# Projecting pairs of weight chunks by seven block products instead of eight in a three-branch decoder layer

## The chip, the cores and the metric

The kernel runs on one core of one Trainium2 chip. The metric is the time of one execution on the device in microseconds (us); lower is better. Engines are named as the profile names them: PE is TensorE's matmuls (PEld its weight loads), DVE is VectorE, ACT is ScalarE, POOL is GpSimd, SP is the engine from whose queue nearly all DMAs are issued.

## The reference

One decoder layer on 2048 tokens of width 1024, with 16 meta tokens in front: three causal mixers with four heads of 128 side by side, each gated and projected back.

```python
xn = rms_norm(h, norm_w)
proj = jnp.einsum('btd,dn->btn', xn, w_in)          # 1024 -> 9224 columns
(sb_q, sb_k, sb_v, sb_z, gd_qkv, gd_z, gd_b, gd_a,
 hg_q, hg_f, hg_i, hg_z, mix) = jnp.split(proj, split_points, axis=-1)
...
o_sb = stick_breaking_attention(q, k, v, valid) * silu(sb_z)
o_gd = rms_norm(gated_delta_rule_chunked(l2_norm(gq), l2_norm(gk), gv, beta, g)) * silu(gd_z)
o_hg = rms_norm(hgrn2_chunked(silu(hg_q), hk, hg_i, log(forget))) * silu(hg_z)
y = sum over b of sigmoid(mix[b]) * (o_b @ w_branch[b])
return h + y @ w_out
```

All inputs are float32.

## The kernel before, in words

The 2048 tokens are worked through in four quarters of 512 columns (`TQ`); the first also carries the 16 meta tokens (`META`), so its tiles are 528 wide (`WQ`). Activations lie with features on the partitions: eight tiles of 128 features for the normed input.

*Dense work* is a Python generator (`dense_work`). For each quarter it projects 73 chunks of 128 output columns of `w_in` (`proj`): per head four for the attention (k, q, v, gate), one small chunk for beta and decay (`CH_BA`), twelve convolved ones and four gates for the delta rule, sixteen for HGRN2, and 24 mix gates, the latter mixed with the branch products (`branch`: four heads x 1024 outputs for each of three branches). At the end stands the output projection (`outp`, eight chunks).

Each float32 operand is held as a high and a low part of type float32r, and a product of two is three matmuls (`mm3`: high x high, high x low, low x high, lines 147 to 149). A chunk is 8 x 3 matmuls of 512 columns into one PSUM bank; in the first quarter, chunks that also need the meta tokens run in two halves of 264. Weights come from HBM in blocks of 128 x 512 (`load_w`): in the first quarter the raw block is loaded, ACT casts the high part (line 136), DVE or POOL subtracts to get the low part (line 110), and both parts are stored to a DRAM scratch (`wk`, 512 KB); later quarters read that (line 132). The tiles for it are `w2` (five buffers) and `wraw` (two).

*Scans* are generators too: the attention scan per head (`sb_scan`), preparation and scan of the delta rule (`gdn_mats`, `gdn_scan`), and the HGRN2 scan, two heads at a time (`hg_scan`). `weave` runs a scan beside a number of dense steps; both yield estimates of time, by which it interleaves them. `later` puts small follow-up steps of a projection (transposes, sums over features) behind the next chunk. The order so written is the priority order of the tile scheduler, which sets each engine's final sequence and the buffers; each engine then runs its sequence in order, waiting on semaphores.

PSUM has eight banks: three for `acc` (dense work), four for `z` and `tr` (scans), one for `av` (the attention's accumulator). SBUF's wide tiles come in tags: `D` (18 buffers, dense results), `S` (21, scans), `g`, `y`, `ob`. The gated sum `y` over the branches stays in SBUF between branches.

## Time and profile before

| | |
|---|---|
| median of 3 runs | 2871.85 us (2870.64 to 2877.4) |
| the profiled execution's own time | 2878.11 us |
| its span, first to last instruction | 2876.0 us |
| instructions | 42134 |
| granted TensorE clock, mean | 0.993 |
| DMA, packets and data | 198288 packets, 522.74 MB |
| HBM | 399.13 MB read, 120.84 MB written |

Busy time of an engine is the sum of its instructions' durations; matmuls are pipelined, so that of PE overlaps itself, and the rate of matmuls is read from the spacing of their starts. A window's row gives its length, the busy time of each engine with the instructions in it, the granted clock, the DMA engines' mean busy share and what they moved in GB/s. A row of waits reads: who, at which line, waited for whom; us in total, how many times, the longest. A row of a group reads: line, engine, operation, out<-in, shapes, count, then busy us and mean ns of one, then the engine's idle time before them and what ended it.

### The profile page before, as it was taken

The page shows a single profiled execution, that of the slowest core. Times are in us where ns is not written, and L with a number is a line of the kernel's source. Part 1 is how long each engine was busy: PE and PEld are TensorE (multiplying, and loading weights), DVE is VectorE, ACT ScalarE, POOL GpSimd, SP SyncE. Part 2 cuts the span into 40 slices and gives each one's busy share as a digit, 9 for nine tenths or more (in the row PEclk, how much of TensorE's full clock was granted, in tenths as well). Part 3 has the DMA queues.
Part 4 walks back from the last instruction along what each step waited for, and adds up shares of the span by engine and source line. Part 5 has one row for each costly group of instructions (what it writes and reads, how often), then busy time and mean ns, then how long its engine had stood idle before and what let it go on. Part 6 is the DMA issues. An engine that isn't in the chain of part 4 may idle for free.

```text
span 2876.0 us, 42134 instructions
## 1 busy us (share of the span) xinstructions
PE 2786.5 (97%) x15691; PEld 2325.4 (81%) x15691; DVE 1524.5 (53%) x3069; ACT 932.1 (32%) x2123; POOL 760.0 (26%) x1012
## 2 busy tenths in 40 slices
PE   5999999998999999999999999999999999999999
PEld 4898788886788888888888888888888777787887
DVE  4467637635257543654156855555415677627521
ACT  4555233333245312113045531211314555121110
POOL 4556213333123401212022421111302233302111
PEclk9999999999999999999999999999999999999999
DMA  6667655667754664446754456344674443653546
GB/s 203 237 214 230 230 193 189 227 233 260 252 170 148 193 181 133 139 153 226 227 190 163 155 161 186 106 142 147 227 227 147 141 139 125 197 155 103 155 153 212
DMA packets 198288, 522.74 MB, mean 182 GB/s; under 512 B 40448, under 2 KB 41536, under 8 KB 198084
## 3 DMA queue, kind: packets, MB, share of 16 engines
q1 hardware_dynamic: 197796, 519.98, 55.6%
q8 instruction: 124, 2.03, 0.3%
q14 instruction: 80, 0.66, 0.1%
q10 hardware_dynamic: 288, 0.07, 0.0%
HBM read 399.13 MB, written 120.84 MB: 181 GB/s over the span
## 4 chain that ended last, share of the span: by engine, by line
PE 81%; DVE 7%; DMA 6%; ACT 2%; POOL 2%; issue 1%; SPq 1%; ACTq 0%; DVEq 0%; POOLq 0%
PE acc L147 21%; PE acc L149 21%; PE acc L148 20%; DMA wraw<-in_w_in_dram 2%; PE z L1011 2%; PE tr L445 2%; PE acc L276 1%; PE av L147 1%; PE av L148 1%; PE av L149 1%; PE z L147 1%; PE z L149 1%; PE z L148 1%; DVE D L178 1%; DMA wraw<-in_w_out_dram 1%
## 5 line engine op out<-in xcount | busy, mean ns | idle before, releaser
L147 PE MATMUL acc<-xh,w 128*128 128x512 f32 (+1 forms) x2568 | 989.8, 386 | 15.4 <-ACT w L136 4.1
L149 PE MATMUL acc<-xh,w 128*128 128x512 f32 (+1 forms) x2568 | 974.6, 380 | 0.4 <-POOL w L110 0.4
L148 PE MATMUL acc<-xl,w 128*128 128x512 f32 (+1 forms) x2568 | 966.6, 376 | 7.9 <-DVE xl L110 7.9
L147 PEld LDWEIGHTS acc<-xh,w 128*128 128x128 f32 x2568 | 486.9, 190 | 97.0 <-ACT w L136 4.2
L148 PEld LDWEIGHTS acc<-xl,w 128*128 128x128 f32 x2568 | 487.5, 190 | 88.1 <-DVE xl L110 8.4
L149 PEld LDWEIGHTS acc<-xh,w 128*128 128x128 f32 x2568 | 485.6, 189 | 85.6 <-POOL w L110 0.8
L110 POOL TENSOR_TENSOR w<-wraw,w 128x512 fp32r<-128x512 f32 x110 | 145.4, 1323 | 346.7 <-ACT w L136 327.9
L136 ACT CAST w<-wraw 128x512 fp32r<-128x512 f32 x186 | 115.0, 618 | 251.9 <-DMA wraw<-in_w_in_dram 104.8
L421 POOL TENSOR_TENSOR S<-S,S 128x256 f32<-128x256 f32 (+2 forms) x108 | 95.2, 882 | 382.9 <-DVE S L413 217.5
L413 DVE TENSOR_TENSOR_SCAN S<-S,cc,zero 128x272 f32<-128x272 f32 (+2 forms) x152 | 144.1, 948 | 82.2 <-ACT S L407 81.7
L147 PE MATMUL acc<-ob,w 128*128 128x512 f32 x384 | 156.4, 409 | 11.9 <-DVE D L1083 5.5
L407 ACT ACTIVATE S<-z,rq 128x128 f32<-128x128 f32 (+4 forms) x216 | 116.8, 541 | 129.1 <-PE z L149 95.2
L148 PE MATMUL acc<-ob,w 128*128 128x512 f32 x384 | 153.4, 400 | 0.0
L149 PE MATMUL acc<-ob,w 128*128 128x512 f32 x384 | 152.3, 397 | 0.0
L592 DVE SCALAR_TENSOR_TENSOR D<-D,cw,D 128x512 f32<-128x512 f32 (+1 forms) x144 | 125.2, 869 | 23.1 <-ACT D L590 20.7
L110 DVE TENSOR_TENSOR S<-tr,S 128x512 fp32r<-128x512 f32 (+4 forms) x176 | 105.1, 606 | 39.8 <-ACT S L449 39.1
L1085 POOL TENSOR_TENSOR y<-y,g 128x512 f32<-128x512 f32 x32 | 49.7, 1558 | 285.8 <-DVE g L1083 285.8
L1067 ACT ACTIVATE g<-acc 128x512 f32<-128x512 f32 x64 | 38.3, 598 | 261.9 <-PE acc L149 247.2
L116 POOL TENSOR_SCALAR nu<-nv 128x8 f32<-128x8 f32 (+4 forms) x40 | 15.3, 383 | 397.2 <-DVE nv L888 231.1
L408 ACT ACTIVATE S<-z,rq 128x128 f32<-128x128 f32 (+4 forms) x216 | 116.3, 538 | 0.0
L449 ACT CAST S<-tr 128x512 fp32r<-128x512 f32 (+4 forms) x176 | 91.0, 529 | 59.4 <-PE tr L445 58.1
L445 PE MATMUL tr<-ident,S 128*128 128x128 f32 (+1 forms) x608 | 100.9, 273 | 3.9 <-POOL S L421 3.2
(325 smaller groups left out, 4700.7 us busy)
## 6 DMA issues: line engine op xcount, KB each, us to landing
w<-wk SPq DMA_DIRECT2D x558, 512.0 KB, 3.5
wk<-w SPq DMA_DIRECT2D x186, 512.0 KB, 2.9
wraw<-in_w_in_dram SPq DMA_DIRECT2D x146, 256.0 KB, 3.8
D<-in_xq_dram SPq DMA_DIRECT2D x56, 256.0 KB, 4.7
S<-rows SPq DMA_DIRECT2D x48, 256.0 KB, 4.5
S<-dv SPq DMA_DIRECT2D x48, 256.0 KB, 4.5
out_dram<-D SPq DMA_DIRECT2D x32, 256.0 KB, 4.7
S<-dk SPq DMA_DIRECT2D x24, 264.0 KB, 4.0
```

Source lines behind the costliest of these rows:

```text
L110: (eng or nc.gpsimd).tensor_sub(out_, a, hi.bitcast(F32))
L136: nc.scalar.copy(hi, raw)
L147: nc.tensor.matmul(dst, lh, rh, start=first, stop=False)
L148: nc.tensor.matmul(dst, lh, rl, start=False, stop=False)
L149: nc.tensor.matmul(dst, ll, rh, start=False, stop=last)
L407: nc.scalar.activation(pc[:, :n], z[:, :n], AF.Sigmoid, scale=rq[:, NT + i : NT + i + 1])
L408: nc.scalar.activation(at[:, :n], z[:, :n], AF.Sigmoid, scale=rq[:, i : i + 1])
L413: nc.vector.tensor_tensor_scan(pc[:, 0:n][:, ::-1], pc[:, 0:n][:, ::-1], zero1.broadcast_to([P, n]), 1.0 if carry[i] is None else carry[i] ...
L421: eng.tensor_mul(at[:, :n], at[:, :n], pc[:, 1 : n + 1])
L445: nc.tensor.transpose(tr[:kw, i * P : (i + 1) * P], ats[i][:, a - lo : a - lo + kw], ident)
L449: nc.scalar.copy(ath[:kw, cs_], tr[:kw, cs_])
L592: nc.vector.scalar_tensor_tensor(dst[:, c0:], raw[:, c0 + i : c0 + i + n], cw[:, ci, i : i + 1], dst[:, c0:], ALU.mult, ALU.add)
```

## The change

*Pairs of chunks in later quarters.* `proj` is replaced by `proj2`, which takes two chunks a and b. Seen as a product of 2 x 2 blocks (inputs 0 to 511 and 512 to 1023; chunk a and chunk b; tokens in two halves of 256), it needs eight block products. In quarters two to four seven are made, by Winograd's scheme: of blocks of weights 11, 12, 22 and four sums of blocks S1 to S4, with blocks of the input 11, 21, 22 and four sums t1 to t4. Each product is 4 x 3 matmuls of 256 columns into its own PSUM bank, with its own weight tile.

*Sums.* `norm_x` makes the input's sums once per quarter and splits all seven blocks. `sums_w` makes S1 to S4 in the first quarter, after a pair has been projected plainly (`proj2_plain`, eight products in halves of 264 for all chunks), and stores their high and low parts. Blocks 11, 12 and 22 are stored only for the attention and delta-rule chunks (`all_kept`); for the others later quarters load them raw and split them again, on ACT and POOL.

*Evacuation.* The products are combined out of PSUM: one ACT copy, then DVE additions (`total`, `sum_to`) into small tiles `u` (256 columns, five buffers); activations then read those. Some gate multiplications and scalings go to POOL.

*Buffers.* PSUM: four banks for `acc`, and `av` shares the four of `z`. SBUF: one set of 47 wide slots serves `D`, `S`, `g`, `y` and `ob`; `y` goes to DRAM and back between branches; the delta rule's inversion takes a `w2` tile and a `u` tile, its output reuses `gq`; HGRN2's `AT` tiles come from the slots.

*Order.* `later` takes the number of ticks after which a step is due; the attention's keys and values of an earlier quarter are fetched one quarter ahead; the small chunk holds its high and low parts side by side in one weight tile and uses two matmuls per block; the counts and costs for `weave` are new.

```diff
-    ps_acc = ctx.enter_context(tc.tile_pool(name="ps_acc", bufs=3, space=PSUM))
+    ps_acc = ctx.enter_context(tc.tile_pool(name="ps_acc", bufs=4, space=PSUM))
     ps_z = ctx.enter_context(tc.tile_pool(name="ps_z", bufs=4, space=PSUM))
-    ps_av = ctx.enter_context(tc.tile_pool(name="ps_av", bufs=1, space=PSUM))
...
+    WIDE = {"D", "S", "g", "y", "ob"}
+    N_WIDE = 47
...
+    def pair_w(ca, cb, j):
+        a1, a2, b2 = w_in[ca][:, :512], w_in[ca][:, 512:], w_in[cb][:, 512:]
+        for src, key in ((a1, "11"), (a2, "12"), (None, "S2"), (None, "S3"), (None, "S1"), (b2, "22"), (None, "S4")):
+            key = (ca, key)
+            yield parts(kept_w(key) if key in kept else split_w(w_raw(src), j))
...
+    def sums_w(ca, r11, r12, r21, r22):
+        w_eng(0).tensor_add(r22, r21, r22)
+        w_eng(0).tensor_sub(r21, r11, r21)
+        w_eng(0).tensor_sub(r11, r22, r11)
+        w_eng(0).tensor_sub(r12, r12, r11)
+        for i, (name, v) in enumerate((("S3", r21), ("S1", r22), ("S2", r11), ("S4", r12))):
+            w2 = spare(4 + i % 2)
+            nc.scalar.copy(w2[:, 0], v)
+            sub_lo(w2[:, 1], v, w2[:, 0], w_eng(0))
+            d_ = dram.tile([P, 2, 512], F32, name=nm("wk"))
+            nc.sync.dma_start(d_, w2.bitcast(F32))
+            kept[ca, name] = d_
...
+    def proj2(j, xs, ca, cb, meta, eva, evb, mid=True):
...
+        def prod(dst, name):
+            wh, wl = nxt[0]
+            nxt[0] = next(gen, None)
+            xh, xl = xs[name]
+            for k in range(4):
+                mm3(dst, wh[:, k], wl[:, k], xh[:, k], xl[:, k], k == 0, k == 3)
...
+        ps = bank()
+        yield from prod(ps, "11")
+        p1 = side()[:, :n]
+        nc.scalar.copy(p1, ps)
+        p2 = bank()
+        yield from prod(p2, "21")
+        give(eva, p1, p2, ha)
+        p6 = bank()
+        yield from prod(p6, "t2")
+        u2 = total(p1, p6)
+        p7 = bank()
+        yield from prod(p7, "t3")
+        u3 = total(u2, p7)
...
+        yield from prod(p5, "t1")
+        give(evb, u3, p5, hb)
+        nc.vector.tensor_add(u2, u2, p5)
+        p4 = bank()
+        yield from prod(p4, "t4")
+        give(evb, u3, p4, ha)
+        p3 = bank()
+        yield from prod(p3, "22")
+        give(eva, u2, p3, hb)
```

Three places in the third quarter's second branch show what moves; names are tiles with their numbers. First PE, at the first mix gates, before: one chunk, `acc_18329` its bank, `w` a weight tile, `xh` and `xl` the input's parts.

```order
L147 MATMUL acc_18329<-xh_13558,w_3822_18325 128x512
L148 MATMUL acc_18329<-xl_13559,w_3822_18325 128x512
L149 MATMUL acc_18329<-xh_13558,w_3822_18325 128x512
L147 MATMUL acc_18329<-xh_13563,w_3822_18325 128x512
L148 MATMUL acc_18329<-xl_13564,w_3822_18325 128x512
L149 MATMUL acc_18329<-xh_13563,w_3822_18325 128x512
```

The same engine and place now, from the end of the fifth of the seven products on:

```order
L230 MATMUL acc_24368<-xh_17876,w_4916_24352 128x256
L228 MATMUL acc_24390<-xh_17882,w_4920_24371 128x256
L229 MATMUL acc_24390<-xl_17883,w_4920_24371 128x256
L228 MATMUL acc_24408<-xh_17874,w_4923_24391 128x256
L229 MATMUL acc_24408<-xl_17875,w_4923_24391 128x256
L230 MATMUL acc_24408<-xh_17874,w_4923_24391 128x256
L228 MATMUL acc_24408<-xh_17874,w_4923_24391 128x256
```

Matmuls are half as wide, a bank and a weight tile change after twelve of them, and the sixth product, whose weights are split again from a raw block (`w_4920`), is left after two matmuls for the seventh and finished after it.

Then DVE, at the same gates, before (lines 981 to 1020 are the HGRN2 scan; the gate itself is evacuated by ACT, and L1083 multiplies a branch product by it):

```order
L981 TENSOR_TENSOR S_18543<-D_18218,D_18183 128x32x8
L985 TENSOR_TENSOR S_18570<-D_17882,S_18379 128x16x16
L1019 TENSOR_TENSOR S_18416<-S_18416,D_18183 128x32x8
L981 TENSOR_TENSOR S_18570<-D_18008,D_17881 128x16x16
L1083 TENSOR_TENSOR g_18324<-g_18324,acc_18355 128x512
```

and now:

```order
L349 TENSOR_TENSOR u_24331<-u_24314,acc_24316 128x256
L349 TENSOR_TENSOR u_24349<-u_24314,acc_24334 128x256
L349 TENSOR_TENSOR u_24366<-u_24349,acc_24351 128x256
L349 TENSOR_TENSOR u_24386<-u_24366,acc_24368 128x256
L412 TENSOR_TENSOR u_24349<-u_24349,acc_24368 128x256
L1246 TENSOR_TENSOR S_24461<-D_23521,D_23782 128x256
L1246 TENSOR_TENSOR S_24498<-D_23946,D_24139 128x256
L349 TENSOR_TENSOR u_24405<-u_24366,acc_24390 128x256
L349 TENSOR_TENSOR u_24421<-u_24349,acc_24408 128x256
```

Seven additions out of PSUM stand on DVE for one pair, each freeing a bank (two for the fifth product's), with scan operations among them.

Last the SP queue, before: both blocks of the branch's weights, of the first gate's chunk and of the second's:

```order
L132 DMA w_3819_18320<-wk_5173 128x1024
L132 DMA w_3820_18322<-wk_5180 128x1024
L132 DMA w_3822_18325<-wk_5188 128x1024
L132 DMA w_3823_18327<-wk_5195 128x1024
L132 DMA w_3833_18393<-wk_5266 128x1024
L132 DMA w_3834_18395<-wk_5273 128x1024
```

and now (`wraw` are raw blocks):

```order
L135 DMA wraw_24291<-in_w_in_dram 128x512
L135 DMA wraw_24297<-in_w_in_dram 128x512
L154 DMA w_4883_24168<-wk_6168 128x1024
L135 DMA wraw_24369<-in_w_in_dram 128x512
L154 DMA w_4886_24189<-wk_6158 128x1024
L154 DMA w_4889_24206<-wk_6163 128x1024
L154 DMA w_4897_24252<-wk_6173 128x1024
L135 DMA wraw_24516<-in_w_in_dram 128x512
L135 DMA wraw_24522<-in_w_in_dram 128x512
L154 DMA w_4910_24317<-wk_6314 128x1024
```

A pair of these gates takes three raw blocks and four kept ones where two chunks took four kept ones, and the raw blocks of a pair are issued ahead of the kept blocks of the pair before it.

In whole programs: 6312 matmuls of 128x512 on `xh` and `xl` give way to 9072 of 128x256 (and 60 + 60 for the small chunk), those of 128x264 go from 1392 to 3456 (and 32); 756 additions out of `acc` come to DVE; POOL gets 289 more splits and sums of 128x512 weights, DVE 195 more, ACT 340 more casts of weights; reads of `wk` go from 558 to 681, raw loads of `w_in` from 146 to 200 plus 72 of double size, stores to `wk` from 186 to 227, and y adds 64 stores and 64 loads of 256 KB.

654 lines of the change are left out of this document (411 added, 243 removed).

## The prediction

> **What bounds the kernel now.** First the page: span, busy time, queues, chain.
>
> ```profile
> span 2876.0 us, 42134 instructions
> PE 2786.5 (97%) x15691; PEld 2325.4 (81%) x15691; DVE 1524.5 (53%) x3069; ACT 932.1 (32%) x2123; POOL 760.0 (26%) x1012
> ...
> q1 hardware_dynamic: 197796, 519.98, 55.6%
> ...
> PE 81%; DVE 7%; DMA 6%; ACT 2%; POOL 2%; issue 1%; SPq 1%; ACTq 0%; DVEq 0%; POOLq 0%
> ```
>
> TensorE is busy 97% of the span and carries 81% of the chain; DVE is next, and the DMA queue is busy for 55.6%. So the sum is one of TensorE's instructions, and then of how often it waits. Busy time of a matmul overlaps the next one, so I take spacings of starts from the timeline (start, duration).
>
> ```profile
> 999.67 0.39 PE L147 MATMUL acc<-xh,w 128*128 128x512 f32 x1
> ...
> 1002.21 0.39 PE L149 MATMUL acc<-xh,w 128*128 128x512 f32 x1
> ...
> 160.53 0.28 PE L147 MATMUL acc<-xh,w 128*128 128x264 f32 x1
> ...
> 161.99 0.28 PE L147 MATMUL acc<-xh,w 128*128 128x264 f32 x1
> ...
> 1600.36 0.28 PE L147 MATMUL z<-S,D 128*128 128x256 f32 x1
> 1600.48 0.28 PE L148 MATMUL z<-S,D 128*128 128x256 f32 x1
> 1600.60 0.28 PE L149 MATMUL z<-S,D 128*128 128x256 f32 x1
> ```
>
> Eleven steps of 512 columns take 2.54 us, 0.2309 each; twelve steps of 264 take 1.46 us, 0.1217 each, although each has its own weight load; two steps of 256 in the attention scan take 0.24 us. Half the columns cost half the time: weight loads do not show. By quarter (columns: length, then busy PE, PEld, DVE, ACT, POOL, clock, DMA share, GB/s):
>
> ```profile
> 0.00:760.00 760.00, 699.28 (x4351) 602.62 (x4352) 411.12 (x804) 295.93 (x666) 288.61 (x317) 0.99 0.67 225
> 760.00:1440.00 680.00, 677.72 (x3709) 561.55 (x3708) 342.48 (x715) 193.79 (x454) 146.81 (x217) 1.00 0.55 177
> 1440.00:2160.00 720.00, 712.83 (x3865) 589.07 (x3864) 381.54 (x773) 220.41 (x501) 162.38 (x244) 0.99 0.53 170
> 2160.00:2876.00 716.00, 696.65 (x3772) 572.13 (x3770) 389.37 (x778) 221.96 (x504) 162.20 (x234) 0.99 0.48 153
> ```
>
> In the three later quarters TensorE is idle 29 us of 2116; no other resource is above 56%.
>
> **The change part by part.** *Matmuls of the later quarters.* A pair of chunks was 2 x 24 matmuls of 512 columns, 48 x 0.2309 = 11.08 us. It becomes 7 products x 12 matmuls of 256 columns. For their spacing the bounds are 0.1155 (half of 0.2309) and 0.120 (the attention rows); I take 0.1185, near the 264 row scaled by columns (0.1180). 84 x 0.1185 = 9.95 us, 1.13 less (bounds 1.38 and 1.00). There are 36 pairs in each of three quarters: 108 x 1.13 = 122 us less (149 to 108).
>
> *Matmuls of the first quarter.* It keeps eight products, but all chunks now run in two halves of 264. 44 of the 72 ran with 512: 48 x 0.1217 - 24 x 0.2309 = 0.30 us more each, 13 us. *The row chunk (CH_BA)*: 24 x 0.2309 = 5.54 becomes 40 x 0.1185 = 4.74 in later quarters, and 48 x 0.1217 becomes 32 x 0.1217 in the first: 4 us less. Branch products, output projection and scans keep their matmuls. TensorE's sum: -122 + 13 - 4 = -113 us (-140 to -99).
>
> *Evacuation.* Rows that price the new work of the other engines:
>
> ```profile
> L110 DVE TENSOR_TENSOR S<-tr,S 128x256 fp32r<-128x256 f32 x16 | 6.6, 414 | 1.1 <-ACT S L449 1.1
> L110 DVE TENSOR_TENSOR w<-wraw,w 128x512 fp32r<-128x512 f32 x76 | 56.3, 741 | 75.9 <-ACT w L136 75.5
> L136 ACT CAST w<-wraw 128x512 fp32r<-128x512 f32 x186 | 115.0, 618 | 251.9 <-DMA wraw<-in_w_in_dram 104.8 <-PE acc L149 48.8 <-DMA wraw<-in_w_out_dram 28.2
> L110 POOL TENSOR_TENSOR w<-wraw,w 128x512 fp32r<-128x512 f32 x110 | 145.4, 1323 | 346.7 <-ACT w L136 327.9 <-DMA wk<-w 14.8 <-PE acc L160 2.8
> DVE S L413 <- ACT S L407: 119.0, 61, 5.8
> ```
>
> A later pair adds 7 DVE additions out of PSUM, 7 x 0.414 = 2.9 us, 313 us over 108 pairs, all beside TensorE. With the first quarter's block sums and splits (195 more 128x512 operations at 0.741 us, 144 us) DVE comes to about 2000 us, 71%. POOL gets 289 more operations of 1.32 us and smaller ones (about 1230 us in all), ACT 340 more casts of 0.62 us (about 1200). All fit by average, so their work costs nothing; what can cost is lateness. A PSUM bank was filled for 5.5 us and two others stood by, so an evacuation could be 11 us late; now a bank is filled for 12 x 0.1185 = 1.42 us and three stand by, 4.3 us. DVE was itself held by ACT 61 times in the scan, up to 5.8 us. The places are windows in which DVE is already full; sixteen 40 us windows have it at 28 us or more, the first, the fullest but one and the last being:
>
> ```profile
> 200.00:240.00 40.00, 37.77 (x313) 37.02 (x313) 31.50 (x41) 20.77 (x48) 27.43 (x32) 1.00 0.67 207
> 2280.00:2320.00 40.00, 37.70 (x192) 29.30 (x191) 33.97 (x63) 24.70 (x52) 16.89 (x27) 1.00 0.28 93
> 2680.00:2720.00 40.00, 40.00 (x190) 32.93 (x190) 29.53 (x69) 4.95 (x10) 10.31 (x14) 1.00 0.60 180
> ```
>
> Two and a half pairs in such a window bring DVE 7 us more. TensorE lost 0 to 2.3 us in each of these three; I add 1.5 us to each of sixteen, 24 us (0 to 80: at most 5 us each, the part of 34 + 7 that passes 36). A gap costs more than itself:
>
> ```profile
> 2320.99 0.36 PE L147 MATMUL av<-S,D 128*128 128x256 f32 x1
> 2324.34 0.39 PE L148 MATMUL av<-S,D 128*128 128x256 f32 x1 [2.99 <-DVE S L110]
> ...
> 2324.92 0.54 PE L148 MATMUL acc<-xl,w 128*128 128x512 f32 x1
> ...
> 2328.24 0.48 PE L147 MATMUL acc<-xh,w 128*128 128x512 f32 x1
> ```
>
> After 2.99 us of waiting for DVE nine matmuls took 3.32 us in place of 9 x 0.2309 = 2.08: 1.2 us on top. With four such gaps more, 5 us, the term is 29 us. The Trainium skill ("TensorE: Matmul & The Clock Gate", Part 1) says that the array falls to half clock after an idle window of about 3.4 us; the trace agrees in kind, with a gap that is a little shorter. By that rule shorter gaps would cost only themselves, and the term would be 24.
>
> *Weights.* A later pair read 4 blocks of 512 KB (2.10 MB). Fourteen pairs of each quarter now read 7 (3.67 MB), 22 read 4 such and 3 raw blocks of 256 KB (2.88 MB). With the first quarter's stores and y through DRAM (128 x 256 KB) the total rises from 520 to about 691 MB. The rate:
>
> ```profile
> 720.00:760.00 40.00, 39.36 (x173) 31.55 (x174) 6.54 (x12) 5.96 (x10) 4.95 (x5) 1.00 0.83 284
> 0.00:260.00 260.00, 221.01 (x1559) 201.62 (x1560) 142.91 (x259) 131.74 (x289) 140.76 (x180) 1.00 0.65 218
> SPq L132 <- PE acc L149: 1532.1, 495, 16.1
> PE z L147 <- DMA S<-dk: 0.3, 1, 0.3
> ```
>
> 284 GB/s at a share of 0.83 is 342 at a full share; 691 MB are 2020 us, 72% of the new time. Before, the queue waited for TensorE to free buffers, 1532 us in all: transfers came early. Now a seven-block pair needs 3.67 / 0.342 = 10.7 us where nothing else runs on TensorE, 0.8 more than its matmuls. Nothing else runs in the first 2.5 pairs of a later quarter: 7.5 x 0.8 = 6 us; elsewhere scans stretch the pair (all 42 would be 33). The Trainium skill ("DMA: Bandwidth & Descriptors", "Where 436 GB/s comes from") gives 425 GB/s measured for one core; by that estimate the pair needs 8.6 us and the 6 us go. No 40 us window shows above 284, so I keep 342. In the first quarter a stored pair moves 4.72 MB, 13.8 us against 96 x 0.1217 = 11.7; its first 260 us move 57 MB, now 79, 230 us at 342: 89% full. I add 10 us (0 to 14 x 2.1 = 29).
>
> *Splits of raw blocks.* POOL's 1.32 us per block fits in 1.42, hidden by the four raw buffers; uncovered it would be 0.62 + 1.32 - 1.42 = 0.52 us for each of 198 blocks, 103. I take 0 as ACT and POOL are under a third busy there. *The rest at nothing, with its cover:* norm_x of a later quarter (28 casts, 28 splits and 16 subtractions of 256 columns; 16 and two thirds of 28 on DVE, 35 x 0.414 = 14 us) lies under the 192 output matmuls, 44 us; attention keys and values fetched one block ahead save nothing, since TensorE waited 0.3 us for them (last row above); the accumulator in the four z banks, four short scans for one long one and a slower inversion buffer lie on engines with room (0 to 20).
>
> The sum, against the profiled execution: 2878.1 (span 2876.0 and 2.1 around it) - 113 + 29 + 6 + 10 = 2810; that execution lies 6.3 us above the median 2871.85, so 2804 on the median's scale.
>
> **The rivals.** *Evacuation becomes the bound (slower).* At each pair DVE is held once by an unfinished scan step, as in the waits row (119.0 / 61 = 1.95 us), and four banks do not cover it: 108 x 1.95 = 211, 2871.85 - 113 + 211 = 2970. It decides from 1.05 us a pair on. For it: 4.3 us of cover against waits up to 5.8. Against: in most waits TensorE has scan work, and the mean is under half the cover. Chance 0.09. *Raw splits show (slower):* 2804 + 103 = 2907, 0.03. *Weights become the bound in every seven-block pair:* 33 + 29 in place of 6 + 10, 2850; 0.12. *Every wait stays covered:* 2871.85 - 113 = 2759; for it, TensorE waits for 29 us in 2116 now; against it the thinner cover; 0.14. *The forecast*, most of the gain and 45 us of new waits: 0.62, its own range 2765 to 2845.
>
> **How the numbers follow.** A measurement of this kernel can tell about 0.3%, 8.6 us. Faster: 0.59 of the forecast, 0.14, and 0.09 of the weights' case, 0.82; same: 0.03 and 0.03, 0.06; slower: 0.12. The range goes down to the full gain with the best spacing and 20 us of waits (2871.85 - 140 + 20 = 2752) and up to the least gain with 102 us of waits (2875); outside lie the slower cases and a few hundredths below.
>
> **What would show it.** Spacing of 256-column matmuls near 0.1185 in the timeline; in the waits, TensorE held by DVE additions (the new u tiles) for under 60 us, and by weight tiles for under 30; a DMA share of 0.70 to 0.75 with about 691 MB; DVE busy near 2000 us. Wrong it would be made by a spacing of 0.13 or more, by clocks below 0.97 in the later quarters, or by DVE's adds standing behind scan steps that come late.

## The result and the profile after

The changed kernel takes 2940.73 us (median of four runs, 2935.04 to 2943.93) against 2871.57 of the kernel before on the same chip: 1.0234 times as long, interval 1.0212 to 1.0257. The prediction was 2804 (2752 to 2875) and 0.82 for faster. It is slower, and outside the range.

The page of the profiled execution, the same lines that were shown of before:

```profile
span 2942.2 us, 56367 instructions
PE 2730.8 (93%) x20667; PEld 2538.6 (86%) x20667; DVE 2056.0 (70%) x4138; ACT 1167.5 (40%) x2800; POOL 1301.3 (44%) x1465
...
q1 hardware_dynamic: 257988, 691.45, 69.5%
...
PE 54%; DVE 23%; DMA 9%; issue 5%; POOL 5%; ACT 3%; SPq 1%; POOLq 0%; DVEq 0%; ACTq 0%
```

TensorE's busy time fell by 56 us and the span rose by 66. TensorE carries 54% of the chain in place of 81%; VectorE went from 7 to 23%, DMA from 6 to 9%. Bytes, VectorE's 2056 us and the DMA share of 69.5% came out near what was worked out beforehand. So did the step of a narrow matmul; from the timeline (start, duration):

```profile
1500.10 0.28 PE L230 MATMUL acc<-xh,w 128*128 128x256 f32 x1
...
1504.86 0.28 PE L228 MATMUL acc<-xh,w 128*128 128x256 f32 x1
```

Forty steps in 4.76 us are 0.119 each. The work is as short as forecast, and the time went elsewhere. A quarter ends with its eighth output addition. The end of a quarter divides the windows below; the first four rows are of before, the other four of the changed kernel (length, busy PE, PEld, DVE, ACT, POOL, clock, DMA share, GB/s):

```profile
0.00:738.30 738.30, 677.58 (x4252) 584.92 (x4253) 408.89 (x799) 293.07 (x661) 286.69 (x315) 0.99 0.66 224
738.30:1408.00 669.70, 667.82 (x3659) 553.44 (x3658) 339.21 (x708) 189.71 (x445) 145.45 (x214) 1.00 0.55 177
1408.00:2118.80 710.80, 703.63 (x3819) 581.70 (x3818) 376.98 (x765) 216.32 (x493) 159.57 (x238) 0.99 0.53 171
2118.80:2876.00 757.20, 737.44 (x3966) 605.32 (x3964) 399.42 (x798) 233.00 (x524) 168.30 (x245) 0.99 0.49 155
```

```profile
0.00:821.00 821.00, 714.33 (x5296) 661.54 (x5297) 613.39 (x1048) 376.84 (x881) 469.77 (x429) 0.96 0.66 239
821.00:1490.50 669.50, 641.22 (x4973) 600.36 (x4972) 450.87 (x992) 241.16 (x604) 261.81 (x329) 0.99 0.75 249
1490.50:2202.40 711.90, 673.77 (x5132) 627.93 (x5131) 491.13 (x1047) 268.22 (x652) 284.44 (x353) 0.98 0.72 237
2202.40:2942.20 739.80, 701.47 (x5275) 648.79 (x5273) 500.57 (x1052) 281.31 (x663) 285.32 (x354) 0.98 0.67 222
```

The first quarter is 83 us longer. The other three hardly moved (to their last addition, 3 us ahead of the end, 669.7, 710.8 and 754.2 became 669.5, 711.9 and 736.8), although 122 us of matmuls left them.

To see where it went I split TensorE's time by the distance from each start to the next. Each form has a step at full clock (0.0580 us for 64 columns, 0.108 for 128, 0.1185 for 256, 0.1217 for 264, 0.2309 for 512 and so on). What goes beyond the step is a *wait* if the profile has the engine idle over 40 ns there, *slow clock* if several steps in a row are over 1.35 times as long, and *rest* otherwise (mostly some 0.16 us by which the step into a wait is longer than the wait).

| us | steps at full clock | waits | slow clock | rest | sum |
|---|---|---|---|---|---|
| before, first quarter | 643 | 47 | 20 | 14 | 724 |
| after, first quarter | 655 | 94 | 41 | 19 | 808 |
| before, three later ones | 2051 | 25 | 31 | 27 | 2133 |
| after, three later ones | 1927 | 101 | 46 | 44 | 2117 |

The steps fell by 112.7 us in all (2694.0 to 2581.3; predicted 113). Waits rose by 123, slow clock by 35, the rest by 22. The prediction had 45 for these together.

No single wait is large. TensorE's longest groups in the later quarters (total, times, longest):

```profile
PE acc L228 <- DMA w<-wk: 19.4, 24, 3.2
PE acc L228 <- DVE u L349: 13.0, 6, 3.7
PE tr L474 <- DVE D L1156: 9.9, 3, 3.3
PE acc L228 <- DVE D L356: 9.7, 6, 4.1
PE z L228 <- DMA S<-dk: 7.5, 4, 3.9
```

The list tells who came last, not what made it late, which took experiments.

### The profile page after: what moved, and what is told of

Same layout as the page of the kernel before. It is cut to its first block, busy times and chain, and to the rows that moved or that the text cites. A ratio compares the mean times of both kernels' runs of the same rounds, so it can differ in the third digit from the quotient of the medians.

```text
span 2942.2 us, 56367 instructions
## 1 busy us (share of the span) xinstructions
PE 2730.8 (93%) x20667; PEld 2538.6 (86%) x20667; DVE 2056.0 (70%) x4138; ACT 1167.5 (40%) x2800; POOL 1301.3 (44%) x1465
## 3 DMA queue, kind: packets, MB, share of 16 engines
q1 hardware_dynamic: 257988, 691.45, 69.5%
## 4 chain that ended last, share of the span: by engine, by line
PE 54%; DVE 23%; DMA 9%; issue 5%; POOL 5%; ACT 3%; SPq 1%; POOLq 0%; DVEq 0%; ACTq 0%
PE acc L228 13%; PE acc L229 13%; PE acc L230 13%; DMA w<-wk 3%; DVE D L828 2%; PE tr L644 2%; DVE w L113 2%; DVE S L612 1%; DMA wk<-sw 1%; DVE w L1017 1%; PE z L1276 1%; POOL w L113 1%; DMA S<-dk 1%; DVE sw L113 1%; PE av L229 1%
## 5 line engine op out<-in xcount | busy, mean ns | idle before, releaser
L228 PE MATMUL acc<-xh,w 128*128 128x256 f32 (+1 forms) x4176 | 1217.4, 292 | 56.9 <-DMA w<-wk 14.0
L230 PE MATMUL acc<-xh,w 128*128 128x256 f32 (+1 forms) x4176 | 1206.1, 289 | 6.8 <-DVE w L113 5.3
L229 PE MATMUL acc<-xl,w 128*128 128x256 f32 (+1 forms) x4176 | 1202.4, 288 | 7.0 <-DVE xl L113 7.0
L228 PEld LDWEIGHTS acc<-xh,w 128*128 128x128 f32 x4176 | 805.6, 193 | 74.3 <-DVE u L349 14.3
L229 PEld LDWEIGHTS acc<-xl,w 128*128 128x128 f32 x4176 | 805.3, 193 | 12.4 <-DVE xl L113 7.3
L230 PEld LDWEIGHTS acc<-xh,w 128*128 128x128 f32 x4176 | 802.8, 192 | 11.3 <-DVE w L113 6.2
L113 POOL TENSOR_TENSOR w<-wraw,w 128x512 fp32r<-128x512 f32 (+1 forms) x216 | 292.5, 1360 | 358.6 <-ACT w L144 311.8
L349 DVE TENSOR_TENSOR u<-u,acc 128x256 f32<-128x256 f32 x504 | 208.5, 415 | 216.6 <-PE acc L230 197.3
L606 ACT ACTIVATE S<-z,rq 128x128 f32<-128x128 f32 (+4 forms) x216 | 116.1, 537 | 123.1 <-PE z L230 107.0
L194 ACT CAST sw<-sw 128x512 fp32r<-128x512 f32 x144 | 88.8, 621 | 147.0 <-DMA wk<-sw 58.5
L828 DVE SCALAR_TENSOR_TENSOR D<-D,cw,D 128x512 f32<-128x512 f32 (+1 forms) x144 | 128.3, 915 | 4.1 <-ACT D L826 3.9
L113 POOL TENSOR_TENSOR w<-sw,w 128x512 fp32r<-128x512 f32 x62 | 91.1, 1483 | 78.4 <-ACT w L144 70.0
L113 POOL TENSOR_TENSOR sw<-sw,sw 128x512 fp32r<-128x512 f32 x60 | 91.0, 1521 | 70.0 <-ACT sw L194 69.9
```

Of the source, the lines that this page charges most:

```text
L113: (eng or nc.gpsimd).tensor_sub(out_, a, hi.bitcast(F32))
L194: nc.scalar.copy(w2[:, 0], v)
L228: nc.tensor.matmul(dst, lh, rh, start=first, stop=False)
L229: nc.tensor.matmul(dst, lh, rl, start=False, stop=False)
L230: nc.tensor.matmul(dst, ll, rh, start=False, stop=last)
L349: nc.vector.tensor_add(v, x, y)
```

## The experiments

Each kernel is judged by its ratio to before, and by the ends of its quarters: since the quarters follow one another, an edit of the first and one of the later quarters can share a run. "Later quarters" is the sum of the three to their last addition: 2134.7 us before, 2118.2 after. Each such figure is of one execution. Where runs share the changed kernel's code, first quarters lie between 818.9 and 825.8 us and later ones between 2110.2 and 2123.1, so differences of under some 10 us tell little.

**Where the time lies: sums, frame, weights, order.** Four kernels, each made from the changed one (`...` marks lines left out).

*No block sums* (no_sums):

```diff
-        sums_w(ca, raws[ca, 0], raws[ca, 1], raws[cb, 0], raws[cb, 1])
+        some = next(iter(kept.values()))
+        for name in ("S1", "S2", "S3", "S4"):
+            kept[ca, name] = kept.get((ca, "11"), some)
```

> Leaves out the block sums of the first quarter (four additions, four splits and four stores of each of 36 pairs): the names of the sums point at a block that is there, so the later quarters read as many bytes and the numbers are other ones. Theory A (the first quarter was lengthened by its block sums, which fill VectorE there: 613 us busy of 821): the last output product of the first quarter ends near 755 us in place of 821, the later quarters keep their 669, 712 and 737 within 5 us, and the time is 2876. Theory B (the first quarter was lengthened by fewer slots, half-width banks and another order of the work): it stays above 800 us and the time above 2920.

Measured: 2859.95 us (0.9944 of before, 0.9925 to 0.9962). Its first quarter:

```profile
0.00:735.90 735.90, 689.32 (x5296) 647.36 (x5297) 423.10 (x884) 303.69 (x737) 265.17 (x305) 0.99 0.49 164
```

85 us came out of the first quarter, and the others stayed as they were (667.8, 712.3 and 739.3, 1 us more in all). VectorE lost 190 us of work there, POOL 205, and TensorE's clock returned from 0.96 to 0.99. Theory A holds, and by more than it named (736 us in place of 755): the block sums are the whole lengthening of that quarter. Without them it is 2 us shorter than before, although its own steps are 11 us longer.

*Eight products in the frame of the changed kernel* (plain):

```diff
-        if j == 0:
-            yield from proj2_plain(xs, ca, cb, give, mid, eva, evb)
-            return
+        yield from proj2_plain(j, xs, ca, cb, give, mid, eva, evb)
+        return
...
+                w.append(parts(split_w(raw[:, i], 0, (ch, i)) if j == 0 else kept_w((ch, i))))
...
-        sums_w(ca, raws[ca, 0], raws[ca, 1], raws[cb, 0], raws[cb, 1])
```

> Eight products in all quarters, in two halves of 256 columns, and no block sums; slots, banks, order of the work and the trip of y through DRAM stay as in the changed kernel. TensorE's own sum grows by 108 x 12 matmuls x 0.1185 = 154 us against the changed kernel. Theory A (the new waits come from the sums and from the additions behind seven products): the first quarter loses some 65 us, the later quarters lose most of the 76 us of waits and 15 us of slow clock that they gained: 2941 + 154 - 65 - 91 = 2939. Theory B (the waits come with slots, banks and order): only the additions' and sums' direct work goes, 3030 to 3095. Theory C (the weights' larger traffic made the waits): as A for the later quarters, 2940 to 2960.

Measured: 2871.62 us (0.9986 of before, 0.9975 to 0.9997). The two windows are its second and third quarter:

```profile
726.20:1405.60 679.40, 677.52 (x5396) 643.68 (x5395) 337.03 (x740) 202.12 (x538) 152.73 (x235) 1.00 0.58 185
1405.60:2117.20 711.60, 705.98 (x5556) 666.62 (x5555) 369.37 (x796) 227.70 (x586) 166.56 (x259) 1.00 0.57 182
```

TensorE is busy 677.5 of 679.4 us. Theory B falls: with narrow halves, slots, banks and order cost nothing. The time is also some 67 us below what theories A and C named. TensorE's steps are 38 us longer than before's (2732 against 2694), since narrow halves cost more than wide chunks, and yet the time is the same: the frame gained some 40 us, which the prediction had put at nothing. What in the frame gained them was not taken apart; with wide chunks the same frame loses (see below). And the run shows how little the seven products bring: 2140.8 us in the later quarters with eight, 2118.2 with seven, 23 us for 151 us of steps.

*Weight blocks read by half* (light):

```diff
-        nc.sync.dma_start(w2.bitcast(F32), kept[key])
+        nc.sync.dma_start(w2[:, 0].bitcast(F32), kept[key][:, 0])
+        light.append(w2)
...
+        if light and light[-1] is w2:
+            return [v.rearrange("p (k c) -> p k c", c=P) for v in (w2[:, 0], wlo)]
```

> Stored weight blocks are read back with their high half alone, 256 KB in place of 512; one fixed low half stands in for all (the numbers are other ones, the matmuls as many). Traffic of the later quarters falls by about 45%. Theory C (the weights' traffic stands behind most new waits of the later quarters, also where another engine ended them): 90 us less, 2850. Theory A (VectorE's queue stands behind most of them): only the waits that the trace puts down to weight tiles and attention tiles go, 20 + 8 us, and some 8 us of slow clock after them: 2905. The first quarter, whose blocks are made and not read, stays at 821.

Measured: 2917.0 us (1.0139, 1.0124 to 1.0154). The queue's total fell from 691 to 514 MB, the later quarters from 2118.2 to 2092.7: 25 us. The time is nearer to theory A's 2905 than to C's 2850: 25 us is about what the trace puts down to weight and attention tiles (19.4 and 7.5), and far from the 90 of theory C.

*The convolution's operations spread* (spread). The chain of work in the second quarter pointed at them:

```profile
1064.23 0.33 DVE u L349
1064.56 3.02 DVE D L828 x2
1067.58 0.39 DVE D L486
1067.97 0.66 DVE D L828
1068.64 0.34 DVE u L349
1069.02 0.58 PE acc L228
```

L349 is the addition that frees an accumulator bank, L828 a tap of the convolution of the pair before: the addition stands behind taps and TensorE behind the addition.

```diff
-        nc.scalar.mul(dst[:, c0:], raw[:, c0 : c0 + n], cw[:, ci, 0:1])
-        for i in range(1, 4):
-            nc.vector.scalar_tensor_tensor(
...
+        bits.append(lambda: nc.scalar.mul(dst[:, c0:], raw[:, c0 : c0 + n], cw[:, ci, 0:1]))
+        for i in range(1, 4):
+            bits.append(lambda i=i: tap(i))
...
             xh, xl = xs[name]
+            bit(3)
```

> The twelve operations of the convolution behind each pair (six of them 0.92 us each on VectorE in a row) are issued three at a time between the products of the next pair, not in one run ahead of them; nothing else changes. Theory A1 (what costs is the order on VectorE: a pair's additions stand behind a run of long operations): the waits of 3 to 4 us at the start of the pairs behind a convolution go, with the slow clock after them: 10 us in each of the three later quarters, some in the first: 2905 to 2915. Theory A2 (what costs is VectorE's amount of work in these stages): within 6 us of the changed kernel's 2941.

Measured: 2950.5 us (1.0264, 1.0247 to 1.028), not better than the changed kernel's 1.0234. The waits moved; TensorE's largest in its later quarters:

```profile
PE acc L229 <- DMA w<-wk: 25.1, 32, 2.2
PE acc L482 <- ACT D L868: 17.9, 3, 6.3
...
PE acc L229 <- DVE u L356: 6.3, 6, 1.9
```

Waits on additions fell from 13.0 to 6.3 us, but the convolution's result now came later, and its reader waited for the new group of 17.9 us. Theory A1 was read from a chain that was right at its place, but this other order gained nothing: it changed who waits.

**What the later quarters give back: additions, cover, banks.**

*No additions, no stores of sums* (noadds_nostore):

```diff
-            d_ = dram.tile([P, 2, 512], F32, name=nm("wk"))
-            nc.sync.dma_start(d_, w2.bitcast(F32))
-            kept[ca, name] = d_
...
-            ev(x, y, a, b)
+            ev(None, y, a, b)
...
-        u2 = total(p1, p6)
+        u2 = None
...
-        u3 = total(u2, p7)
+        u3 = None
...
-        nc.vector.tensor_add(u2, u2, p5)
```

> Two edits that touch different quarters. In the later quarters the additions behind the seven products are left out: each half is evacuated from its last product alone, as one of eight products would be (VectorE loses about 250 of its 1440 us there, TensorE keeps all matmuls; the numbers are other ones). In the first quarter the block sums are made, but their four stores of 512 KB a pair are left out (75 MB of 196). Later quarters, 2118 us now (2141 with eight products in the same frame, where TensorE's own sum is 151 us larger, so that 128 us came back as waits). Theory A (the additions hold TensorE's banks and VectorE's queue): 2050 or less. Theory D (the scans set the pace: their chains of steps are as long as before, and the products between them are now too short to cover them): 2105 or more. First quarter, 821 us now: if the stores' traffic lengthened it, about 750; if the arithmetic of the sums did, 810 or more.

Measured: 2916.47 us (1.0143, 1.0123 to 1.0162). Later quarters 2085.2: the additions cost 33 us, between the bounds of A and D. First quarter 823.9: the stores cost nothing, although the rate fell to 147 GB/s:

```profile
0.00:823.90 823.90, 719.83 (x5295) 665.61 (x5296) 628.67 (x1048) 380.19 (x881) 460.25 (x429) 0.95 0.44 147
```

*Both together, and sums on POOL* (noadds_light_pool): the edits of the last run and of the light weights, and `nc.gpsimd` in place of `w_eng(0)` in `sums_w`.

> Later quarters: the additions left out and, besides, stored weight blocks read back with their high half alone, as in the run with light weights, which took 2093 us for these quarters. Theory A with the weights beside it: both savings add up, 2020 to 2030, near TensorE's own 1927 us and the 63 us that the frame loses with eight products. Theory D: 2080 or more. First quarter: the additions and splits of the block sums all run on POOL, none on VectorE (613 us busy of 821 now, POOL 470). If VectorE's work is what lengthens the quarter, about 775 us; if the sums' chain through ACT and POOL is, 821 or longer.

Measured: 2930.95 us (1.0188, 1.0162 to 1.0214). Later quarters 2061.8, 56 us less than the changed kernel: the savings of 25 and 33 add up. The figure lies between the two theories (2030 and 2080): 2061.8 is still 72 us above the 1990 that these steps (1927) would take with the 63 us that eight products lose. The first quarter grew to 869.2.

*One bank less* (bank3):

```diff
-    ps_acc = ctx.enter_context(tc.tile_pool(name="ps_acc", bufs=4, space=PSUM))
+    ps_acc = ctx.enter_context(tc.tile_pool(name="ps_acc", bufs=3, space=PSUM))
```

> Three accumulator banks in place of four, nothing else. With one bank being filled, evacuation may now be 2 x 1.42 = 2.8 us late in place of 4.3. Theory A2 (evacuations are late all the time, and what cover there is decides): 60 us or more in the later quarters (2118 now). Theory D, or few long waits that no bank would cover: under 15 us there.

Measured: 2980.81 us (1.0354, 1.0334 to 1.0375), 40 us above the changed kernel over all quarters. No trace of an execution of this length was kept, so the quarters can't be told apart, and neither theory is decided by it; only that a bank is worth tens of us and not hundreds.

*One product twice* (eighth):

```diff
-            for k in range(4):
-                mm3(dst, wh[:, k], wl[:, k], xh[:, k], xl[:, k], k == 0, k == 3)
+            n = 8 if name == "22" else 4
+            for i in range(n):
+                k = i % 4
+                mm3(dst, wh[:, k], wl[:, k], xh[:, k], xl[:, k], i == 0, i == n - 1)
                 if k % 2:
-                    yield 2 * CHUNK_US / 14
+                    yield 2 * CHUNK_US / 16
```

> In the later quarters one of the seven products is run twice into the same bank: 96 matmuls a pair again, as with eight products, while weights, additions and order stay those of seven (the numbers are other ones). TensorE's own sum grows by 108 x 12 x 0.1185 = 154 us. Theory D (the scans' chains set the pace and the products between their steps became too short): the added matmuls fill waits, the later quarters take 2118 + 50 to 80, and the time is 2990 to 3020. Theory A with the weights (late additions and late weight blocks cost what they cost, 57 us by the runs without them): a bank is then filled for longer only once a pair, so most waits stay: 2118 + 120 to 154, 3060 to 3095.

Measured: 3038.54 us (1.0554, 1.0521 to 1.0587), between the two. Later quarters 2216.6: 154 us of added steps lengthened them by 98. So 55 us of the matmuls that the change removed had stood where TensorE would have waited anyway: waits fell from 101 to 64 us, slow clock from 46 to 35. Ahead of the scans' tiles (`z`, `tr`, `av`) the waits fell from 39.5 to 18.7 us, ahead of `acc` from 61.4 to 45.0. Its second quarter:

```profile
825.80:1527.70 701.90, 684.79 (x5404) 646.74 (x5403) 445.84 (x992) 240.92 (x604) 259.20 (x329) 1.00 0.72 237
```

The added product stands in one place, at the pair's end; how much cover it would give spread over the pair was not tried.

*The account closed* (eighth_noadds_light): the edits of eighth, of light and of the left-out additions.

> Later quarters with one product run twice (TensorE's matmuls as with eight products), the additions left out and weight blocks read back by half: the three edits together, to close the account. Singly and in pairs they gave, for the three later quarters: 2118 as changed, 2217 with the product run twice, 2062 without additions and with light weights; eight products in the same frame take 2141. If additions and weights cost the same whatever TensorE has to do: 2217 - 56 = 2161. If longer products cover them too: 2185 or more. If they are all that parts the run with the doubled product from eight products: 2141. First quarter 821.

Measured: 2982.18 us (1.0369, 1.0352 to 1.0386). Later quarters 2157.8, first 818.9. Additions and weights cost 59 us with longer products too, as the first of the three theories had it (2161). TensorE is busy again; the second quarter:

```profile
818.90:1503.30 684.40, 680.62 (x5403) 645.16 (x5402) 363.28 (x763) 254.05 (x652) 245.86 (x305) 1.00 0.49 155
```

17 us remain above plain's 2140.8, not much more than two executions differ by; they were not divided further (blocks split anew from raw weights, the longer input step, the order of the pairs).

*Smaller pieces* (fine):

```diff
-                if k % 2:
-                    yield 2 * CHUNK_US / 14
+                yield CHUNK_US / 14
```

> The changed kernel with its seven products handed out between the scans' steps in pieces of 3 narrow matmuls (0.36 us) in place of 6 (0.71 us); nothing else. Theory E (the evenness of the interleaving decides how much of a scan step's latency is covered): the 42 us of waits ahead of scan steps and part of the slow clock go, 2941 - 40 = 2900. Theory D (what lacks is the amount of products between steps): within 10 us of 2941.

Measured: 2954.86 us (1.0261, 1.0232 to 1.0291). Theory E falls; mixing products and scan steps more finely gained nothing.

**By what the sums lengthen the first quarter.** Three kernels: the eight operations one at a time between the next pair's matmuls (sums_spread), all of them on VectorE (sums_dve: `nc.vector` in place of `w_eng(0)`), and the additions without the splits (sums_half).

```diff
 # sums_spread
-        w_eng(0).tensor_add(r22, r21, r22)
...
+            bits.append(lambda op=op, o=o, x=x, y=y: getattr(w_eng(0), "tensor_" + op)(o, x, y))
...
+            bits.append(lambda i=i, name=name, v=v: split_sum(i, name, v))
...
 # sums_half
-        for i, (name, v) in enumerate((("S3", r21), ("S1", r22), ("S2", r11), ("S4", r12))):
...
+        for name in ("S1", "S2", "S3", "S4"):
+            kept[ca, name] = kept.get((ca, "11")) or next(iter(kept.values()))
```

> The four additions and four splits of a first-quarter pair's block sums are issued one at a time between the matmuls of the next pair, in place of all eight in a row behind their own pair; amount and engines stay. Theory G (order: a run of eight sum operations stands on VectorE and POOL ahead of the next pair's weight splits and the scans' steps): the first quarter falls from 821 us by 40 or more. Theory H (amount: VectorE and POOL have no room for 288 more operations beside the scans, wherever they stand): within 12 us of 821.

> All eight operations of a pair's block sums on VectorE (0.74 us each), none on POOL (1.36 us). All on POOL took the first quarter from 821 to 869 us. Theory H1 (VectorE's time is the scarce one, as its 613 us busy suggest): 840 or more. Theory H2 (POOL's slow operations in the chain of sums and in front of weight splits are what hurts): 790 or less.

> Of the block sums only the four additions of a pair are made; the four splits (cast on ACT, subtraction, store) are left out, and the names point at a block that is there. Without any sums the first quarter takes 736 us, with all 821, without the stores alone 824. Theory H (amount): half the operations, half the price, 775 to 785. If the splits carry the price (their chain passes ACT too): 750 or less.

Measured: 2944.84 us (1.0234, 1.0213 to 1.0255), 2922.58 (1.0163, 1.0143 to 1.0184) and 2892.33 (1.0055, 1.0034 to 1.0076). The first quarters, in this order, and behind them that of the run with all sums on POOL:

```profile
0.00:819.10 819.10, 715.31 (x5296) 662.70 (x5297) 619.64 (x1048) 379.35 (x881) 469.82 (x429) 0.96 0.68 240
```

```profile
0.00:800.80 800.80, 708.62 (x5296) 657.10 (x5297) 614.05 (x1172) 378.46 (x881) 321.42 (x305) 0.96 0.69 245
```

```profile
0.00:772.10 772.10, 702.88 (x5296) 656.41 (x5297) 519.63 (x966) 303.75 (x737) 359.25 (x367) 0.97 0.46 156
```

```profile
0.00:869.20 869.20, 730.66 (x5296) 675.92 (x5297) 591.10 (x885) 379.26 (x881) 673.09 (x593) 0.93 0.63 225
```

This other order is worth 2 us, no more than two executions differ by (theory H, amount). Half the operations cost 36 of the 85 us, a little under half. With all sums on VectorE the quarter is 20 us shorter (not the 31 or more that H2 asked for), with all on POOL 48 longer. The sums cost by their amount, and more so on POOL, whose operation takes nearly twice as long. Whether VectorE's time is scarce this does not tell: it has 124 operations more in the second row than in the first and in the changed kernel (x1172 and x1048), and is busy for 614 us in place of 613 in the changed kernel, since its operations got shorter as POOL did less (last section).

**Is there a faster version?** The frame had gained 40 us with narrow halves, so wide chunks in it promised more. *Wide chunks in the frame* (wide: plain, with both halves of the input side by side in one tile; the edit is shown against plain), and the same in smaller pieces (wide_fine):

```diff
-            for half, rng in enumerate(halves(j)):
+            for rng in halves(j) if j == 0 and meta else [(META, WQ)]:
                 ps = p_acc()[:, : rng[1] - rng[0]]
...
```

> The kernel before's products in the changed kernel's frame: eight products in all quarters, chunks of 512 columns in one bank wherever no meta columns are read (44 chunks of the first quarter, all of the later ones), no block sums. Against the run with eight products in halves TensorE's own sum falls by 108 x (11.38 - 11.08) = 32 us and 13 us in the first quarter: 2872 - 45 = 2827, if the slots, the order of the work and the additions moved off VectorE gain what that run says (45 us against before at equal products). If wide chunks need the slack that narrow ones leave between their evacuations, 2860.

> As the run with chunks of 512 columns, but the products are handed out between the scans' steps in pieces of 3 wide matmuls (0.69 us), as the kernel before did and as 6 narrow ones take, in place of 6 wide ones (1.39 us). That run took 2961 where 2827 was expected; its waits of 86 us in the later quarters stand ahead of scan steps for three quarters (66 us), against 18 us in all with narrow chunks. Theory E (the size of the pieces made these waits): 2827 within 12 us. Theory F (wide chunks hold a bank, or the scans' banks, too long in this frame): 2930 or more.

Measured: 2961.13 us (1.0293, 1.0276 to 1.031) and 2959.33 (1.0284, 1.0255 to 1.0312). The sum was off by 134 us, and the size of the pieces isn't the reason (theory E). TensorE's two largest groups of waits in the later quarters of wide are for scan steps:

```profile
PE tr L641 <- POOL S L617: 17.6, 13, 2.9
PE tr L471 <- DVE D L1153: 15.9, 3, 5.3
```

*Narrow matmuls evacuated late* (late): plain, with both halves of a later chunk in one bank, evacuated together; the edit is shown against plain.

```diff
+            one = p_acc() if j else None
...
-                give(ev, None, ps, rng)
+                if j == 0:
+                    give(ev, None, ps, rng)
+                elif half:
+                    give(ev, None, one, (META, WQ))
```

> Eight products in halves of 256 columns as in the run that took 2872, but both halves of a later chunk go into one bank and are evacuated together at the chunk's end, as a wide chunk is; matmuls and pieces stay. Theory J (a result that comes out whole, half a chunk later and in operations twice as long, is late for the chain behind it: the 90 us that wide chunks lost): 2940 or more. If the width of the matmuls itself is what the scans suffer from: within 15 us of 2872.

Measured: 2894.95 us (1.0071, 1.0056 to 1.0085): its later quarters are 24 us longer than plain's, wide's 86. Neither theory holds, and what the other 62 us are stays open. *Wide chunks for the gates alone* (gates_wide), whose results are read much later; the edit is shown against wide:

```diff
-            for rng in halves(j) if j == 0 and meta else [(META, WQ)]:
+            for rng in halves(j) if meta else [(META, WQ)]:
...
-                        if k % 2:
-                            yield CHUNK_US / (8 if j == 0 and meta else 4)
+                        if k % 2 or not meta:
+                            yield CHUNK_US / 8
```

> Eight products in the changed kernel's frame, chunks of 512 columns for the 28 gate chunks of a quarter alone (their results are read much later), halves of 256 or 264 for the 44 others, from which norms, convolutions and scans follow at once. TensorE's own sum is 14 pairs x 0.30 = 4 us smaller a later quarter and 8 us in the first than with halves throughout: 2872 - 21 = 2851, below the kernel before, if wide chunks cost nothing where no chain waits for them. If wide chunks cost waits wherever they stand: 2890 or more.

Measured: 2865.43 us (0.9969, 0.9956 to 0.9981), 6 us below plain where 21 us of steps went. Of the versions that compute the layer it is the fastest that was run: by some 75 us against the changed kernel and by 0.3% against the one before, with eight products.

## Why the prediction was wrong

From the kernel before to the changed one, to the last addition (2873.0 to 2939.2 us), by the runs; rows of 10 us and under, and in part the last one, are no larger than two executions differ by:

| what | measured us | by | predicted |
|---|---|---|---|
| frame: slots, banks, order, with 38 us of steps more for narrow halves | -6 | plain | +13 - 4, the rest 0 |
| first quarter, rest | +10 | no_sums against plain | 0 |
| block sums | +85 | no_sums | 10 (their traffic) |
| steps of the seven products | -154 | their count x 0.1185 | -122 against wide chunks |
| matmuls that had covered waits | +55 | eighth | none |
| additions and weights | +59 | eighth_noadds_light | 29 + 6 |
| remainder of the later quarters | +17 | the same against plain | 0 |

*TensorE's sum* was right: -113 predicted, -112.7 found, with the step of 0.119 us.

*"All fit by average, so their work costs nothing; what can cost is lateness."* This is the step that failed most. VectorE at 71% and POOL below a half were taken to hide 288 sum operations in the first quarter. They cost 85 us, and another order of them gained nothing. With them VectorE is busy for 613 and POOL for 470 of 821 us, so neither was full; what failed is the step from room on an engine to cover for its work. Weight splits, norms and scan steps, for all of which TensorE waits, stand in the same two queues. TensorE's waits in that quarter rose from 47 to 94 us; some of their rows now (a weight split, a step of the delta rule's preparation, a gate, a step of the attention scan):

```profile
PE acc L230 <- DVE w L113: 7.0, 6, 2.4
PE z L951 <- DVE S L936: 5.8, 2, 5.2
PE acc L889 <- DVE D L486: 5.7, 1, 5.7
PE tr L644 <- DVE S L620: 5.7, 2, 4.2
```

That each sum operation delays what stands behind it is my reading of it; shown is that the price goes with their number and with the engine. The prediction also gave VectorE's operations one price whatever POOL does, and with the sums on POOL they grew (last section). The 10 us that it did add there, for the stores' traffic, were wrong too: leaving the stores out shortened nothing.

*The sum takes the whole -122 off the time.* TensorE's 97% busy was read as a bound. Of the 154 us of steps that seven products save against eight in halves, 55 had stood where TensorE would otherwise wait: about half of that ahead of the scans' tiles, by the waits of eighth, and the rest ahead of `acc`, where what was late stays open. It was not late additions and weights, which cost 59 us with longer products and 56 without. The prediction asked what would be late next of evacuation and weights; the scans' work it counted only as cover for these.

*Additions:* 29 us predicted, 33 found in the later quarters (with their slow clock). The size was near; where in a quarter they are lost, in the sixteen full windows or elsewhere, no run separates. *Weights:* 6 predicted, inside its bounds of 0 to 33, 25 found. Around the end of the first quarter the DMA share reached this:

```profile
800.00:840.00 40.00, 36.79 (x214) 32.78 (x213) 10.45 (x20) 4.89 (x11) 1.48 (x2) 0.96 0.98 360
```

360 GB/s at a share of 0.98 is 367 at a full one, above the 342 that I scaled from. The Trainium skill ("DMA: Bandwidth & Descriptors", "Where 436 GB/s comes from") has 425 GB/s for one core; no 40 us window of the changed kernel came near it, but over 3.41 us (174.49 to 177.90) it moved 414.

*The rivals.* "Evacuation becomes the bound" named 2970, near the result, but not by its mechanism: it had additions late by 1.95 us in each of 108 pairs, 211 us, and without any additions 33 us went. "Weights become the bound in every pair" had the size of the weights' term right (33 us beside 25). No rival had the cover that removed matmuls gave, or the first quarter's arithmetic. "The rest at nothing": the frame, with narrow halves, gained about 40 us at equal steps, the one term that went better than forecast.

*The signs that were named* did not warn: spacing 0.119, VectorE 2056 us, waits on weight tiles 19.4 us (under 30), waits on additions under 60, clocks 0.98 and 0.99 in the later quarters, a DMA share of 0.695 where 0.70 was named. All of them held or nearly so, and the kernel was slower; none of them looked at the first quarter or at cover. The last sign, additions behind scan steps that come late, was met only in kind: the chain shows them behind the convolution's taps, and spreading those gained nothing.

## What to carry to other kernels

Work that is done once still has to fit where it is done: take the busy share of the quarter, not of the run, and count every queue that it passes. Even that does not price it: VectorE was at 57% of the first quarter without the sums and at 75% with them, and a run without them told what they cost. When matmuls are taken out of a schedule that weaves them between the steps of a scan, part of what is saved can be cover; add dummy matmuls, or take some away, to learn how much before building the rest. A wait's releaser in the trace is only the one that came last: when the convolution was spread, the next one showed.

## What was not expected of the hardware

The slow clock follows waits much shorter than those of the prediction, and not after each. From the timeline of the first quarter (start, duration, idle before), and windows (columns as above):

```profile
171.31 0.59 PE L228 MATMUL acc<-xh,w 128*128 128x264 f32 x1 [1.91 <-DVE cc L617]
171.69 0.42 PE L229 MATMUL acc<-xl,w 128*128 128x264 f32 x1
171.91 0.42 PE L230 MATMUL acc<-xh,w 128*128 128x264 f32 x1
...
174.53 0.28 PE L230 MATMUL acc<-xh,w 128*128 128x264 f32 x1
174.65 0.28 PE L228 MATMUL acc<-xh,w 128*128 128x264 f32 x1
...
237.09 0.50 PE L229 MATMUL av<-S,D 128*128 128x512 f32 x1 [2.60 <-DVE S L113]
```

```profile
167.66:171.07 3.41, 1.60 (x13) 1.00 (x10) 3.41 (x5) 0.64 (x2) 1.39 (x2) 1.00 0.79 238
171.07:174.49 3.42, 3.18 (x14) 3.18 (x15) 2.38 (x7) 1.47 (x4) 3.42 (x3) 0.50 1.00 396
232.51:235.92 3.41, 1.98 (x16) 1.70 (x15) 3.41 (x5) 0.76 (x2) 3.36 (x5) 1.00 1.01 412
235.92:239.34 3.42, 2.25 (x13) 1.48 (x13) 3.42 (x7) 1.57 (x4) 0.64 (x1) 1.00 0.08 31
```

After 1.91 us without work the steps are 0.22 us in place of 0.12 for about 3 us, and the granted clock is 0.50; after 2.60 us it stays at 1.00. The difference goes with where a wait lies. In the trace of the changed kernel all stretches of halved clock begin on one grid of intervals of 3.41 us, and each lasts one or more of them. The shorter wait lay almost wholly in one interval, in which TensorE was busy for 1.60 us; the longer one fell across two, with 1.98 and 2.25 us busy. From 38 us on, all 21 intervals at full clock with 1.9 us or more without work were followed by a halved one, and of those with less than 1.6 us a single one. The Trainium skill ("TensorE: Matmul & The Clock Gate", Part 1) gives an idle window of about 3.4 us for the fall to half clock and a busy one of the same length for the return; the length agrees with the grid here, but a window that was about half idle was enough. Altogether 123 us of new waits came with 35 us of slow clock and 22 us of longer steps into the waits, nearly half on top.

The other is that POOL's work lengthens VectorE's. The 36 taps of the convolution in the first quarter are the same operation in each kernel; without sums, with all sums on VectorE, as changed, and with all on POOL (the last two figures ahead of the idle time are busy us and mean ns of one):

```profile
L830 DVE SCALAR_TENSOR_TENSOR D<-D,cw,D 128x528 f32<-128x528 f32 x36 | 33.2, 933 | 4.8 <-ACT D L828 4.5
L828 DVE SCALAR_TENSOR_TENSOR D<-D,cw,D 128x528 f32<-128x528 f32 x36 | 30.0, 845 | 0.7 <-ACT D L826 0.6
L828 DVE SCALAR_TENSOR_TENSOR D<-D,cw,D 128x528 f32<-128x528 f32 x36 | 40.1, 1125 | 4.1 <-ACT D L826 3.9
L835 DVE SCALAR_TENSOR_TENSOR D<-D,cw,D 128x528 f32<-128x528 f32 x36 | 47.8, 1342 | 1.3 <-ACT D L833 0.8
```

With all sums on POOL, VectorE has one operation more in that quarter than without any sums (885 and 884), and is busy for 591 us in place of 423. In the changed kernel's first quarter its 128x512 subtractions with a float32r result took 0.67 to 0.69 us where no POOL instruction ran beside them, and up to 1.79 us where one did. So all sums on POOL made the first quarter 48 us longer, and all on VectorE made it 20 us shorter, although VectorE had been busy for three quarters of it and POOL for little over half: busy time alone didn't tell which engine had room.
